# A decoder trunk's ConvFFN: up-projection chunks 2 and 3 as a pair by seven products, and its input sums from other engines

## The chip, the cores and the metric

The kernel runs on one core of one Trainium2 chip. The metric is the device time of one execution in microseconds (us), as the median of several runs. A core has five engines that run at the same time, each through its own list of instructions in order: TensorE (PE; its weight loads are shown as PEld), VectorE (DVE), ScalarE (ACT), GpSimd (POOL) and SyncE (SP, which here issues the loads by DMA). GpSimd issues DMAs too, some of which add what they carry to what stands at the destination.

## The reference

The model has two layers over a residual stream of 512 positions by 1024 features (dilated attention, then forgetting attention). The change touches the ConvFFN that ends each layer:

```python
def conv_ffn(xn, w_up, cw, cb, w_down):      # xn: 512 x 1024, w_up: 1024 x 5632
    a = xn @ w_up
    T = a.shape[1]
    ap = jnp.pad(a, ((0, 0), (CONV_W - 1, 0), (0, 0)))
    a = sum(ap[:, j:j + T] * cw[j] for j in range(CONV_W)) + cb
    gate, val = jnp.split(a, 2, axis=-1)      # 2816 columns each
    return (jax.nn.gelu(gate, approximate=True) * val) @ w_down
...
        f = conv_ffn(rms_norm(h, g[2]), w_up[l], conv_w[l], conv_b[l], w_down[l])
        h = h + rms_norm(f, g[3])
```

## The kernel before

**Precision.** Every operand of a matmul is split into a high part and a low part, and each product is three matmuls (`mm3`, L288 to L290): high by high, high by low, low by high. For the transposed input these are `xbh` and `xbl` (in layer 1 `xch` and `xcl`), for a weight block the two halves of a tile `w`. The high part is a cast on ScalarE. The low part is a subtraction on VectorE (L76 in the class `Weights`, L712 in `Pair.low`), or, where `added` is set (L707, L708), ScalarE writes the negated block and a DMA of GpSimd adds the raw block to it. That DMA is called the accumulating DMA below.

**Up-projection.** Its 5632 columns are worked on as 22 chunks; chunk c has 128 gate and 128 value columns. A chunk's two results (128 columns by 512 positions) stand in two PSUM banks. Then follow the taps of the convolution (`tap`, ScalarE L623 and two operations of VectorE), the GELU (L643 on ScalarE), the product of gate and value (L650), and a store of the result `hc` to `hD` in DRAM (L648, issued by GpSimd one chunk later).

Chunks are computed in one of three ways:

- chunks 0 and 1 by `first_products`, at the boundary from the attention. The transposes of the last two blocks of 128 positions (`bd.transpose(2)` and `(3)`) stand between products over 256 positions (`LO`, `HI`), in banks named `first`;
- chunks 2, 3, 20 and 21 directly by `up`: eight steps of 128 rows, three matmuls of 128x512 each;
- chunks 4 to 19 as eight `Pair`s. A pair's weights are four blocks of 512 rows by 256 columns (A11 and A12 from the gate's columns, A21 and A22 from the value's; A11 and A21 for the first 512 features, A12 and A22 for the others), the input four blocks (two halves of its 1024 features by two halves of the positions). Instead of eight products of blocks it takes seven, of sums of blocks: S1 to S4 are sums of the weight blocks, and `XA` and `XB` (`xsh`, `xsl`) hold sums of the input blocks. A product `p_1` to `p_7` is 24 matmuls of 128x256, for two outputs each. `keep_1`, `keep_7` and `keep_2` copy intermediate results from PSUM (ScalarE, L728), and `sum_1`, `sum_3` and `sum_4` add them (VectorE).

**The sums of the input.** `sums_in` adds `xbh` and `xbl` on GpSimd to get the input in float (L660), forms its four sums on VectorE, and then casts to `xsh` and subtracts to `xsl` (L671, L672).

**Order.** The schedule is written out by hand: each engine gets its instructions in the order of the program. In the loop over pairs an iteration runs the pair's products in the order p_7, p_6, p_4, p_5, p_2, p_3, and the next pair's p_1 stands after p_5. While one pair is multiplied, the next pair's blocks are taken from the list of raw loads (`take`), summed (`s1` to `s4`) and split (`high`, `low`). The A11 of a pair is taken and split another iteration ahead (`n2` in the loop). Ahead of the loop stand `sums_in`, chunks 2 and 3, and the first two pairs' first splits.

**Loads.** `Weights` keeps a list of pieces in the order of use, filled by `add_ffn`. SP issues their loads into `wraw` buffers as far ahead as `ahead` (pieces split ahead of use) and `ahead_dma` (pieces loaded ahead of the split) say; there are ten buffers for these and other tiles of that size.

Of the kernel before, what the change touches and what calls it, by code (L numbers as in the profile page):

```python
# [9 lines left out]
F32 = mybir.dt.float32  # L10
# [3 lines left out]
ALU = mybir.AluOpType  # L14

D = 1024
T = 512
NB = 4
KD = D // 128
HD = 64  # L20
DFF = 2816
# [3 lines left out]
BIG = 3.0e38  # L25


PAIRS = tuple(range(4, 20, 2))
ND = NF // 2
LAST = 3  # L30

# [84 lines left out]
def trunk_kernel(ctx, tc, x, norm_gains, w_qkv_a, w_o_a, w_q_b, w_o_b, kv_norm, w_kvf, b_f,  # L116
                 w_up, conv_w, conv_b, w_down, rope, out):
    nc = tc.nc
    act, dve, pool, pe, sp = nc.scalar, nc.vector, nc.gpsimd, nc.tensor, nc.sync
# [8 lines left out]
    def t8(shape, dt=F32, name="t8"):  # L128
        return p8.tile(shape, dt, tag="t8", name=name)
# [52 lines left out]
    def add_ffn(l):  # L182
        for c in range(NF):
            if c in PAIRS:
                for q, f in ((0, 0), (0, DFF), (1, DFF), (1, 0)):
                    add_block(w_up[l], q, f + c * 128)
            elif c - 1 not in PAIRS:
                add_cols(w_up[l], c * 128)
                add_cols(w_up[l], DFF + c * 128)

        for j in range(ND):
            add(lambda raw, j=j: [(raw[:, 0:512], w_down[l][j * 256:j * 256 + 128, 0:512]),
                                  (raw[:, 512:1024], dT[l][j, :, 0:512])])
            add(lambda raw, j=j: [(raw, dT[l][j, :, 512:1536])])
        add_rows(w_down[l], range(1, NF, 2))
# [26 lines left out]
    W = Weights(nc, new_raw, lambda: t8([128, 2, 1024], F32R, name="w"), pieces)  # L222
# [127 lines left out]
        lo = [t8([128, 4, T], F32R, name=f"{name}l{i}") for i in range(2)]  # L350
        return hi, lo

    def transpose_in(b, xn, xT, between=None):

        pts = []
        for i in range(2):
            pt = bank([128, 4, 128], name="xt_ps")
            for k in range(4):
                pe.transpose(pt[:, k, :], xn[:, (4 * i + k) * 128:(4 * i + k + 1) * 128], ident)
            pts.append(pt)  # L360
        s = slice(b * 128, b * 128 + 128)
        for i, pt in enumerate(pts):
            if i and between is not None:
                between()
            hi, lo = xT[0][i], xT[1][i]
            act.copy(hi[:, :, s], pt)
            dve.tensor_tensor(lo[:, :, s], pt, hi[:, :, s].bitcast(F32), ALU.subtract)

    def xs(xT, kc, s):
        return xT[0][kc // 4][:, kc % 4, s], xT[1][kc // 4][:, kc % 4, s]  # L370
# [8 lines left out]
    ALL, LO, HI = slice(0, 512), slice(0, 256), slice(256, 512)  # L379
# [51 lines left out]
    class Boundary:  # L431
# [26 lines left out]
        def transpose(self, b):  # L458
            if self.xT is None:
                self.xT = new_xT(self.name)  # L460
            transpose_in(b, self.xn.pop(b), self.xT)

    class SharedBoundary(Boundary):

# [76 lines left out]
                self.out(b)  # L541


    def first_products(bd, n):
        bd.norm(3)
        outs = [bank([128, T], name="first") for _ in range(n)]
        ws = []
        for i, o in enumerate(outs):
            ws.append(W.get())
            feat_mm(ws[i], bd.xT, o, LO)  # L550
            if i == 0:
                bd.transpose(2)
# [4 lines left out]
        return outs  # L557


    def load_conv(l):  # L560
# [55 lines left out]
    def ffn(l, bd, cp, nxt, gain, ahead):  # L616
# [36 lines left out]
        xT = None  # L653
        XA, XB = [], []

        def sums_in():

            v = [t8([128, 4, T], name=f"xsum{i}") for i in range(2)]
            for i in range(2):
                pool.tensor_tensor(v[i], xT[0][i].bitcast(F32), xT[1][i].bitcast(F32), ALU.add)  # L660
# [4 lines left out]
            dve.tensor_tensor(v[1][:, :, HI], v[1][:, :, HI], v[0][:, :, LO], ALU.subtract)  # L665
            dve.tensor_tensor(v[1][:, :, LO], v[1][:, :, LO], v[1][:, :, HI], ALU.subtract)
            yield
            for X, src in ((XA, v[0]), (XB, v[1])):
                X += [t8([128, 4, T], F32R, name="xsh"), t8([128, 4, T], F32R, name="xsl")]
                for k in (0, 2):  # L670
                    act.copy(X[0][:, k:k + 2], src[:, k:k + 2])  # L671
                    dve.tensor_tensor(X[1][:, k:k + 2], src[:, k:k + 2], X[0][:, k:k + 2].bitcast(F32), ALU.subtract)  # L672
                    yield
# [4 lines left out]
        class Pair:  # L678
# [206 lines left out]
        def run(steps):  # L885
            for _ in steps:
                pass
# [84 lines left out]
        extra = sums_in()  # L972
        next(extra)
        done, last = Chunk(0, first[0:2]), Chunk(1, first[2:4])
        done.taps()
        next(extra)
        done.product()
        last.taps()
        W.ahead, W.ahead_dma = 1, 3
        W.split(base + 7)  # L980
        W.high_added()
        pairs = [Pair(c) for c in PAIRS]
        p, n = pairs[0:2]

        banks = p.new_banks()
        up(W.get(), banks[0], range(KD))
        for _ in range(3):
            next(extra, None)
        p.take("A11", "A21", "A22")
        p.high("A11", True)  # L990
        p.s1()
        p.s3()
        up(W.get(), banks[1], range(KD))
        run(extra)
        p.high("S1", True)
        done, last = last, Chunk(2, banks)

        banks = p.new_banks()
        up(W.get(), banks[0], range(KD))
        done.product()  # L1000
        last.tap(0)
        p.high("S3")
        p.s2()
        last.tap(1)
        p.high("S2")
        last.gelu()
        p.take("A12")
        p.low("S3")
        p.s4()
        up(W.get(), banks[1], range(KD))  # L1010
        p.high("A22", True)
        p.low("S2")
        last.product()
# [893 lines left out]
```

## Time and profile before

| what | before |
|---|---|
| median of 3 runs | 1103.84 us (1103.52 to 1103.93) |
| profiled execution | 1104.32 us |
| its span | 1102.5 us |
| granted TensorE clock, mean | 0.998 |
| chunks 0 and 1 of layer 0, first matmul to the first of chunk 2 | 178.0 to 202.76 us |
| chunk 2's first matmul to p_1 of chunks 4 and 5, layer 0 | 202.76 to 224.55 us |
| GpSimd's sums of the input, layer 0 | 189.53 us, two of 10.19 us together |

The profile shows one execution. Times in it are counted from the span's start. The span is what the profile covers; the execution's own time lies a little above it. A timeline row gives start, duration, engine, line, operation, tiles, shapes and how many were taken together (x2), and in brackets how long the engine sat idle before it and what released it. Matmuls overlap, so a matmul's row lasts longer than the distance to the next. Layer 1's ConvFFN has the same instructions as layer 0's.

### The profile page before, as it was taken

To read this page: it belongs to the slowest core of one execution; us is meant where nothing else is said; L and a number is where in the kernel's file an instruction comes from. 1 tells how busy PE (TensorE), PEld (TensorE's weight loads), DVE (VectorE), ACT (ScalarE), POOL (GpSimd) and SP (SyncE) were. 2 spreads that over 40 slices of the span, in tenths; PEclk is the share of its full clock that TensorE was granted. 3 is DMA by queue.
4 is the path that set the end of the run, shared out by engine and by line. 5 is a ranking of instruction groups with operands and counts; after the bars stand their busy time and mean duration, and the time that the engine had idled before them with its cause. 6 is when DMAs were issued, how large, how long until landed. Compare 5 with 4: busy or idle time off the path is not lost.

```text
span 1102.5 us, 18986 instructions
## 1 busy us (share of the span) xinstructions
PE 1093.6 (99%) x6905; PEld 968.5 (88%) x6905; DVE 892.3 (81%) x1453; ACT 735.1 (67%) x1232; POOL 231.5 (21%) x335
## 2 busy tenths in 40 slices
PE   9999999999999999999999999999999999999997
PEld 6988889899999988888878888889999999988886
DVE  5897788967887789997698677868967887789994
ACT  6754575777788766576562588856677787856572
POOL 2632001322122211000000545600412122211000
PEclk9999999999999999999999999999999999999999
DMA  9699855499999999793447666783499999998872
GB/s 325 184 356 410 317 174 151 91 227 231 224 224 248 230 295 325 277 338 101 134 153 268 210 159 169 216 265 117 98 224 231 231 221 247 224 296 313 317 249 76
DMA packets 156006, 252.06 MB, mean 229 GB/s; under 512 B 12352, under 2 KB 99384, under 8 KB 155912
## 3 DMA queue, kind: packets, MB, share of 16 engines
q1 hardware_dynamic: 137576, 186.61, 51.1%
q0 software_dynamic: 18336, 64.24, 26.3%
q8 instruction: 54, 0.88, 0.3%
q14 instruction: 40, 0.33, 0.1%
HBM read 166.08 MB, written 39.63 MB: 187 GB/s over the span
## 4 chain that ended last, share of the span: by engine, by line
PE 85%; issue 9%; DVE 2%; ACT 2%; DMA 1%; POOL 1%; DVEq 0%; SPq 0%; POOLq 0%; ACTq 0%
PE up L288 12%; PE up L289 12%; PE up L290 12%; PE acc L288 8%; PE acc L290 8%; PE acc L289 8%; PE qk_ps L289 2%; PE qk_ps L288 2%; PE qk_ps L290 2%; PE s_ps L1733 2%; PE o_ps L1781 2%; PE pT_ps L1766 1%; PE first L290 1%; PE first L288 1%; PE first L289 1%
## 5 line engine op out<-in xcount | busy, mean ns | idle before, releaser
L288 PE MATMUL up<-xsh,w 128*128 128x256 f32 x512 | 144.9, 283 | 0.0
L289 PE MATMUL up<-xsl,w 128*128 128x256 f32 x512 | 144.9, 283 | 0.0
L290 PE MATMUL up<-xsh,w 128*128 128x256 f32 x512 | 144.9, 283 | 0.0
L288 PE MATMUL acc<-w 128*128 128x512 f32 (+1 forms) x311 | 120.7, 388 | 0.3 <-DVE mix L337 0.3
L290 PE MATMUL acc<-w 128*128 128x512 f32 (+1 forms) x311 | 120.6, 388 | 0.1
L705 ACT CAST w<-wraw 128x1024 fp32r<-128x1024 f32 x80 | 82.6, 1048 | 37.7 <-DVE wraw L689 37.7
L624 DVE SCALAR_TENSOR_TENSOR bb<-up,conv,bb 128x511 f32<-128x511 f32 x80 | 59.8, 748 | 57.2 <-ACT bb L623 57.0
L289 PE MATMUL acc<-w 128*128 128x512 f32 (+1 forms) x267 | 103.2, 387 | 0.0
L288 PEld LDWEIGHTS up<-xsh,w 128*128 128x128 f32 x512 | 98.3, 192 | 0.0
L289 PEld LDWEIGHTS up<-xsl,w 128*128 128x128 f32 x512 | 98.3, 192 | 0.0
L290 PEld LDWEIGHTS up<-xsh,w 128*128 128x128 f32 x512 | 98.3, 192 | 0.0
L623 ACT ACTIVATE bb<-up,conv 128x512 f32<-128x512 f32 x80 | 60.2, 780 | 32.7 <-DVE up L775 24.3
L288 PE MATMUL up<-xbh,w 128*128 128x256 f32 (+1 forms) x256 | 80.0, 312 | 0.1
L288 PE MATMUL up<-xch,w 128*128 128x256 f32 (+1 forms) x256 | 80.0, 312 | 0.1
L289 PE MATMUL up<-xbl,w 128*128 128x256 f32 (+1 forms) x256 | 79.2, 310 | 0.0
L289 PE MATMUL up<-xcl,w 128*128 128x256 f32 (+1 forms) x256 | 79.2, 310 | 0.0
L290 PE MATMUL up<-xbh,w 128*128 128x256 f32 (+1 forms) x256 | 79.2, 309 | 0.0
L290 PE MATMUL up<-xch,w 128*128 128x256 f32 (+1 forms) x256 | 79.2, 309 | 0.0
L708 POOL DMA_DIRECT2D w<-wraw x48 | 40.4, 841 | 183.5 <-ACT w L707 96.5
L76 DVE TENSOR_TENSOR w<-wraw,w 128x1024 fp32r<-128x1024 f32 x48 | 65.0, 1376 | 11.9 <-ACT w L58 11.4
L58 ACT CAST w<-wraw 128x1024 fp32r<-128x1024 f32 x62 | 63.7, 1051 | 15.8 <-PE v_ps L289 6.9
L290 PEld LDWEIGHTS acc<-w 128*128 128x128 f32 x311 | 58.4, 188 | 12.9 <-DVE w L817 0.9
(308 smaller groups left out, 3279.6 us busy)
## 6 DMA issues: line engine op xcount, KB each, us to landing
wraw<-in_w_up_dram SPq DMA_DIRECT2D x88, 512.0 KB, 6.6
w<-wraw POOLq DMA_DIRECT2D x62, 512.0 KB, 7.6
dT<-dsums SPq DMA_DIRECT2D x28, 512.0 KB, 7.5
dsums<-in_w_down_dram SPq DMA_DIRECT2D x22, 512.0 KB, 7.5
dsums<-in_w_down_dram SPq DMA_DIRECT2D x44, 256.0 KB, 6.6
hD<-hc POOLq DMA_DIRECT2D x44, 256.0 KB, 7.3
wraw<-dT SPq DMA_DIRECT2D x22, 512.0 KB, 6.8
dact<-hD SPq DMA_DIRECT2D x44, 256.0 KB, 5.3
```

Source lines behind the costliest of these rows:

```text
L58: self.nc.scalar.copy(pair[:, 0], raw)
L76: self.nc.vector.tensor_tensor(pair[:, 1], raw, pair[:, 0].bitcast(F32), ALU.subtract)
L288: pe.matmul(o, ah, bh, start=first, stop=False, skip_group_check=shared)
L289: pe.matmul(o, ah, bl, start=False, stop=False, skip_group_check=shared)
L290: pe.matmul(o, al, bh, start=False, stop=last, skip_group_check=shared)
L623: act.activation(bb[:, s, :], ps, AF.Identity, bias=cp[:, 3, ch:ch + 1], scale=cp[:, 2, ch:ch + 1])
L624: dve.scalar_tensor_tensor(bb[:, s, 1:], ps[:, :T - 1], cp[:, 1, ch:ch + 1], bb[:, s, 1:], ALU.mult, ALU.add)
L705: act.copy(w[:, 0], self.f[key])
L708: pool.dma_start(w[:, 1], self.f[key], accum_op=ALU.add)
L1733: pe.matmul(s[hh][:, :nn], qT[j][:, m, hh, i * 128:(i + 1) * 128], k, start=m == 0, stop=m == 1)
L1766: pe.transpose(o[:, k0 + k, :], p[:, hh, k * 128:(k + 1) * 128], ident)
L1781: pe.matmul(o[64 * hh:64 * hh + 64, i * 128:(i + 1) * 128], Vt[hd // 8][:, k, (hd % 8) * 64:(hd % 8) * 64 + 64], pT[j, i, hh][:, k, :], st ...
```

## The change

`PAIRS` starts at chunk 2, so chunks 2 and 3 become a ninth pair, the first. What stood around the direct chunks is written anew:

- the first pair's blocks are loaded in the order A11, A12, A21, A22, and `W.ahead` and `W.ahead_dma` are set after the first product of chunk 0, so that loads for the pairs are asked for from there on;
- the input in float comes from ScalarE, which copies the transposes of blocks 2 and 3 a second time from PSUM (`plain`, L370), and for blocks 0 and 1 from an addition on VectorE (L565);
- the first pair's p_1 and p_2 run right after `first_products`, and its later products in the loop without p_2;
- its S4 is written over the raw block of A12, and chunk 0's GELU and product come after keep_1;
- the second pair's A11 is taken and split in the loop's iteration 0, after the second tap of chunk 1.

```diff
-PAIRS = tuple(range(4, 20, 2))
+PAIRS = tuple(range(2, 20, 2))
...
-                for q, f in ((0, 0), (0, DFF), (1, DFF), (1, 0)):
+                blocks = (0, 0), (0, DFF), (1, DFF), (1, 0)
+                for q, f in blocks if c > PAIRS[0] else (blocks[0], blocks[3], *blocks[1:3]):
                     add_block(w_up[l], q, f + c * 128)
...
+        def plain(v):
+            for t, pt in zip(v, pts):
+                act.copy(t[:, :, s], pt)
+
+        return plain
...
-    def first_products(bd, n):
+    def first_products(bd, n, begin):
...
             if i == 0:
-                bd.transpose(2)
+                W.ahead, W.ahead_dma = 1, 2
+                plain = bd.transpose(2)
+            if i == 1:
+                begin()
+                v = [t8([128, 4, T], name=f"xsum{i}") for i in range(2)]
+                plain(v)
             if i == 2:
-                bd.transpose(3)
+                for t, hi, lo in zip(v, *bd.xT):
+                    dve.tensor_tensor(t[:, :, LO], hi[:, :, LO].bitcast(F32), lo[:, :, LO].bitcast(F32), ALU.add)
+                bd.transpose(3)(v)
...
-            v = [t8([128, 4, T], name=f"xsum{i}") for i in range(2)]
-            for i in range(2):
-                pool.tensor_tensor(v[i], xT[0][i].bitcast(F32), xT[1][i].bitcast(F32), ALU.add)
-            yield
...
-            def s4(self):
-                self.add("S4", "A12", "S2", ALU.subtract)
+            def s4(self, out=None):
+                self.add("S4", "A12", "S2", ALU.subtract, out)
...
-        base = W.n_get
-        first = first_products(bd, 4)
+        pairs = [Pair(c) for c in PAIRS]
+        p = pairs[0]
+
+        def begin():
+            p.take("A11", "A12")
+            p.high("A11", True)
+
+        first, v = first_products(bd, 4, begin)
         xT = bd.xT
...
-        up(W.get(), banks[0], range(KD))
...
-        up(W.get(), banks[1], range(KD))
...
-        n.take("A11")
-        n.high("A11", True)
-        p.p_1()
-        p.keep_1()
-        prev, m = None, [Chunk(3, banks)]
+        sums = sums_in(v)
+        del v
+        W.ahead_dma = 3
+        p.high("A12", True)
+        p.take("A21", "A22")
+        p.s1()
+        p.s3()
+        done, last = Chunk(0, first[0:2]), Chunk(1, first[2:4])
+        p.high("S3")
+        next(sums)
+        p.s2()
+        next(sums)
+        next(sums)
+        p.high("S2")
+        p.low("S3")
+        next(sums)
+        done.tap(0)
+        next(sums)
+        next(sums)
+        p.low("S2")
+        done.tap(1)
+        p.high("A22", True)
+        p.high("S1", True)
+        p.p_1()
+        p.p_2()
+        p.keep_1()
+        done.gelu()
+        p.s4(p.f["A12"])
+        done.product()
+        prev, m = None, [last]
...
             a.tap(0)
-            p.high("A12", True)
+            if prev:
+                p.high("A12", True)
             p.keep_7()
             p.p_6()
             a.tap(1)
+            if not prev:
+                n.take("A11")
+                n.high("A11", True)
...
-            p.p_2()
+            if prev:
+                p.p_2()
```

Two places show what the engines get. The first is ScalarE in layer 0, from the splits of the first pair's last blocks to the S4 of iteration 0. A row is a line, an operation and its tiles; `L713`, `L715` are the casts and negated copies of weight blocks, `L736` the keep copies, `L635` the taps, `L655` the GELU and its table load. After the change:

```order
L713 CAST w<-wsum 128x1024
L715 ACTIVATE w<-wsum 128x1024
L736 COPY csum<-up 128x256 x2
L655 ACT_TABLE_LOAD
L655 ACTIVATE bb<-bb 128x512
L635 ACTIVATE bb<-first,conv 128x512
L736 COPY csum<-up 128x256 x2
L635 ACTIVATE bb<-first,conv 128x512
L713 CAST w<-wraw 128x1024
L715 ACTIVATE w<-wraw 128x1024
L713 CAST w<-wraw 128x1024
```

The first two rows are S1 of the first pair, and the last split with a negated copy is A11 of the second pair; the last row is S4 (written over A12's raw block). The same place before, from the split of S2 to keep_7 of the pair of chunks 4 and 5 (`L705`, `L707` casts and negated copies, `L728` keeps, `L623` taps, `L643` GELU):

```order
L705 CAST w<-wraw 128x1024
L643 ACTIVATE bb<-bb 128x512
L705 CAST w<-wraw 128x1024
L707 ACTIVATE w<-wraw 128x1024
L705 CAST w<-wraw 128x1024
L707 ACTIVATE w<-wraw 128x1024
L728 COPY csum<-up 128x256 x2
L623 ACTIVATE bb<-up,conv 128x512
L705 CAST w<-wraw 128x1024
L707 ACTIVATE w<-wraw 128x1024
L728 COPY csum<-up 128x256 x2
```

Before, the two splits with negated copies ahead of the first keep are the first pair's A22 and the second pair's A11; the one behind it is A12. After the change, the second pair's A11 stands behind keep_1, the GELU, both taps and keep_7.

The second place is GpSimd in layer 0, from the start of the ConvFFN. Before, its list begins with the sums of the input (`xsum`):

```order
L660 TENSOR_TENSOR xsum_2227<-xbh_1858,xbl_1860 128x2048
L660 TENSOR_TENSOR xsum_2228<-xbh_1859,xbl_1861 128x2048
L96 DMA w<-wraw 128x1024
L708 DMA w<-wraw 128x1024
L708 DMA w<-wsum 128x1024
L648 DMA hD<-hc 128x512
L708 DMA w<-wraw 128x1024
L648 DMA hD<-hc 128x512
```

After the change (`L716` the accumulating DMAs, `L660` the stores of `hc`):

```order
L716 DMA w<-wraw 128x1024 x3
L716 DMA w<-wsum 128x1024
L716 DMA w<-wraw 128x1024
L660 DMA hD<-hc 128x512
L716 DMA w<-wraw 128x1024
L716 DMA w<-wsum 128x1024
```

The sums and one accumulating DMA are gone. The first three rows' DMAs are for the first pair's A11, A12 and A22, the next for its S1, and the third row is the second pair's A11, ahead of the first store to `hD`.

More of the change, by code (lines that the diff above doesn't have):

```diff
@@ L351, in new_xT, with transpose_in @@
         return hi, lo
-    def transpose_in(b, xn, xT, between=None):
+    def transpose_in(b, xn, xT):
         pts = []
@@ L664, in sums_in @@
             yield
-            dve.tensor_tensor(v[1][:, :, HI], v[1][:, :, HI], v[0][:, :, LO], ALU.subtract)
-            dve.tensor_tensor(v[1][:, :, LO], v[1][:, :, LO], v[1][:, :, HI], ALU.subtract)
-            yield
             for X, src in ((XA, v[0]), (XB, v[1])):
+                if src is v[1]:
+                    dve.tensor_tensor(src[:, :, HI], src[:, :, HI], v[0][:, :, LO], ALU.subtract)
+                    dve.tensor_tensor(src[:, :, LO], src[:, :, LO], src[:, :, HI], ALU.subtract)
+                    yield
                 X += [t8([128, 4, T], F32R, name="xsh"), t8([128, 4, T], F32R, name="xsl")]
@@ L967, in up @@
                 mm3(o, wh[:, kc, :], wl[:, kc, :], bh, bl, kc == 0, kc == KD - 1)
-        base = W.n_get
-        first = first_products(bd, 4)
-        xT = bd.xT
[L972 to L985, printed above, removed]
-        up(W.get(), banks[0], range(KD))
[L987 to L990, printed above, removed]
+        pairs = [Pair(c) for c in PAIRS]
[4 more added lines that the diff above has]
+        first, v = first_products(bd, 4, begin)
+        xT = bd.xT
+        sums = sums_in(v)
[3 more added lines that the diff above has]
+        p.take("A21", "A22")
         p.s1()
         p.s3()
-        up(W.get(), banks[1], range(KD))
-        run(extra)
-        p.high("S1", True)
-        done, last = last, Chunk(2, banks)
-        banks = p.new_banks()
-        up(W.get(), banks[0], range(KD))
-        done.product()
[L1001 to L1013, printed above, removed]
-        n.take("A11")
-        n.high("A11", True)
-        p.p_1()
-        p.keep_1()
-        prev, m = None, [Chunk(3, banks)]
+        done, last = Chunk(0, first[0:2]), Chunk(1, first[2:4])
[13 more added lines that the diff above has]
+        p.high("A22", True)
+        p.high("S1", True)
+        p.p_1()
[3 more added lines that the diff above has]
+        p.s4(p.f["A12"])
+        done.product()
+        prev, m = None, [last]
         for i, p in enumerate(pairs):
```

8 lines of the change are left out of this document (3 added, 5 removed).

## The prediction

> **What bounds the kernel now.** I read the page's head, busy shares and chain first, then TensorE's own waits, then the timelines of TensorE, ScalarE, VectorE and GpSimd around the place that changes (178 to 240 us in layer 0).
>
> ```profile
> span 1102.5 us, 18986 instructions
> ...
> PE 1093.6 (99%) x6905; PEld 968.5 (88%) x6905; DVE 892.3 (81%) x1453; ACT 735.1 (67%) x1232; POOL 231.5 (21%) x335
> ...
> PEclk9999999999999999999999999999999999999999
> ...
> PE 85%; issue 9%; DVE 2%; ACT 2%; DMA 1%; POOL 1%; DVEq 0%; SPq 0%; POOLq 0%; ACTq 0%
> ```
>
> TensorE is busy for 99% of the span at the full granted clock, and the chain that ends last is TensorE's work and its issue for 94%. The view of waits says what is left to gain by waiting less:
>
> ```profile
> PE warm L248 <- DVE zero L243: 1.2, 1, 1.2
> PE qk_ps L289 <- DVE w L80: 0.3, 1, 0.3
> PE acc L288 <- DVE mix L337: 0.3, 1, 0.3
> ...
> ```
>
> Columns are the waiting tile and line, the releaser, the sum in us, the count and the mean. No row of TensorE names `up` or `first`: nothing in the up-projection is waited for. So ScalarE, VectorE, GpSimd and the queues cost nothing there now, and the time changes only by the matmuls that TensorE no longer runs, and by stalls that the new order brings in.
>
> **Term 1: TensorE's matmuls.** Chunks 2 and 3 are 96 matmuls of 128x512 in each layer; as a pair they are 7 products of 24 matmuls of 128x256. What follows them (p_1 of the next pair) is one more product in both.
>
> ```profile
> 202.76 0.40 PE L288 MATMUL up<-xbh,w 128*128 128x512 f32 x1
> ...
> 224.55 0.28 PE L288 MATMUL up<-xbh,w 128*128 128x256 f32 x1
> ...
> 227.42 0.28 PE L288 MATMUL up<-xsh,w 128*128 128x256 f32 x1
> ```
>
> Rows give start and duration. From the first direct matmul to p_1 are 224.55 - 202.76 = 21.79 us; p_1 takes 227.42 - 224.55 = 2.87 us to the first p_7. Before: 21.79 + 2.87 = 24.66 us. After: 8 x 2.87 = 22.96 us. **1.70 us less per layer, 3.4 in two**, if nothing waits. A whole pair further on gives a lower gain:
>
> ```profile
> 261.86 0.28 PE L290 MATMUL up<-xbh,w 128*128 128x256 f32 x1
> 262.06 0.39 PE L288 MATMUL up<-xbh,w 128*128 128x256 f32 x1
> ...
> 282.40 0.39 PE L288 MATMUL up<-xbh,w 128*128 128x256 f32 x1
> ```
>
> 282.40 - 262.06 = 20.34 us for the seven products, or 2.91 each, which would make it 24.66 - 8 x 2.91 = 1.4 us. But each such start is late by itself (262.06 follows 261.86 by 0.20 instead of 0.12, and lasts 0.39 instead of 0.28), so that pace holds a small stall; I take 2.87 and put the restart (about 0.15) into term 2.
>
> **Term 2: a new wait, of the second pair's p_1.** Before, a pair's A11 was split an iteration ahead. Now the second pair's A11 is split in iteration 0, behind the first pair's keep_1, GELU, keep_7 and both taps on ScalarE. Its low half comes from a chain: ScalarE's cast, ScalarE's negated copy, GpSimd's accumulating DMA. TensorE reads it at the third matmul of p_1, which stands behind six products: due at 202.76 + 6 x 2.87 + 0.24 = 220.22 us. When it is there follows from these rows of ScalarE:
>
> ```profile
> 198.00 1.28 ACT L643 ACT_TABLE_LOAD   x1
> 199.30 0.63 ACT L643 ACTIVATE bb<-bb 128x512 f32<-128x512 f32 x1
> ...
> 227.89 0.78 ACT L623 ACTIVATE bb<-up,conv 128x512 f32<-128x512 f32 x1
> 228.57 1.05 ACT L705 CAST w<-wraw 128x1024 fp32r<-128x1024 f32 x1
> 229.50 1.06 ACT L707 ACTIVATE w<-wraw 128x1024 fp32r<-128x1024 f32 x1
> 230.46 0.64 ACT L728 COPY csum<-up 128x256 f32<-128x256 f32 x2
> 230.98 0.81 ACT L623 ACTIVATE bb<-up,conv 128x512 f32<-128x512 f32 x1
> 231.65 1.07 ACT L705 CAST w<-wsum 128x1024 fp32r<-128x1024 f32 x1
> ...
> 233.65 0.64 ACT L643 ACTIVATE bb<-bb 128x512 f32<-128x512 f32 x1
> 234.18 1.04 ACT L705 CAST w<-wraw 128x1024 fp32r<-128x1024 f32 x1
> ```
>
> What an instruction holds ScalarE for is the distance to the next start: table load 1.30, GELU 0.53, tap 0.68, cast 0.93, two keep copies 0.52 (0.26 each), tap 0.67. The second keep_1 copy reads a bank that p_2 still writes, so it starts after p_2, whose last matmul starts 0.12 before the next product and lasts 0.28: 202.76 + 2 x 2.87 + 0.16 = 208.66. The sum: 208.66 + 0.26 keep + 1.30 table + 0.53 GELU + 0.68 tap + 0.52 keep_7 + 0.67 tap + 0.93 cast + 1.06 negated copy = 214.61, and 0.30 to GpSimd's issue, by this row (229.50 + 1.06 to 230.86):
>
> ```profile
> 230.86 0.84 POOL L708 DMA_DIRECT2D w<-wraw  x1 [5.89 <-ACT csum L728]
> ```
>
> Issue at 214.9. TensorE doesn't wait if the DMA lands within 220.2 - 214.9 = **5.3 us**. The DMA view (last column: us from issue to landing) has the same transfer at 207.10, 236.48, 264.02, 284.36 and 224.12 us:
>
> ```profile
> w<-wraw POOLq DMA_DIRECT2D x1, 512.0 KB, 4.6
> w<-wraw POOLq DMA_DIRECT2D x1, 512.0 KB, 5.6
> w<-wsum POOLq DMA_DIRECT2D x1, 512.0 KB, 6.4
> w<-wsum POOLq DMA_DIRECT2D x1, 512.0 KB, 8.0
> w<-wraw POOLq DMA_DIRECT2D x1, 512.0 KB, 10.0
> ```
>
> The first had the queue to itself. The last was issued 2.1 us behind another accumulating DMA and right behind the store of hD. Here S1's accumulating DMA goes out at about 208.6, some 6 us ahead, raw blocks that come free load beside it, and a store of hD follows right behind: that is nearest to the third row, 0.5 us ahead of a store and 6 us behind another accumulation. **I take 6.4 us**: it lands at 221.3, 1.1 late, and with the restart of 0.15 the stall is 1.25. Ends: 4.6 gives none, 10.0 gives 4.85.
>
> Beside the rows, a rule: the Trainium skill ("DMA: Bandwidth & Descriptors", section "Anatomy of one DMA — SWDGE (gpsimd) path") fits a GpSimd DMA as about 2.0 us plus its bytes over 436e3 per us. For 512 KB my estimate from that page is 3.2 us, which would land at 218.1 with no stall, and the sum would be term 1 alone. The trace speaks against it for this transfer: even the row that was alone took 4.6, and the sum above goes by the rows.
>
> **What I cost at nothing, and its cover.** The x sums move from GpSimd (two adds) to four ScalarE copies and two VectorE adds:
>
> ```profile
> 189.53 10.19 POOL L660 TENSOR_TENSOR xsum<-xbh,xbl 128x2048 f32<-128x2048 f32 x2 [52.12 <-DVE xbl L367]
> 188.76 1.29 DVE L367 TENSOR_TENSOR xbl<-xt_ps,xbh 128x512 fp32r<-128x512 f32 x2 [0.88 <-ACT xbh L366]
> 190.19 5.04 DVE L76 TENSOR_TENSOR w<-wraw,w 128x1024 fp32r<-128x1024 f32 x1
> 188.14 1.08 ACT L366 CAST xbh<-xt_ps 128x512 fp32r<-128x512 f32 x2 [2.52 <-PE xt_ps L359]
> 194.32 0.78 ACT L623 ACTIVATE bb<-first,conv 128x512 f32<-128x512 f32 x1 [4.16 <-PE first L290]
> ```
>
> GpSimd's 10.19 us go, and with them whatever drew VectorE's L76 out to 5.04 us beside them; TensorE waited for neither, so nothing is gained. A pair of ScalarE copies costs about 1.08 (first pair of casts), and lies in gaps of 2.52 and 4.16 us. It matters whether the sums are early enough:
>
> ```profile
> 207.93 2.35 DVE L672 TENSOR_TENSOR xsl<-xsum,xsh 128x1024 fp32r<-128x1024 f32 x2
> ...
> 210.20 1.22 DVE L689 TENSOR_TENSOR wsum<-wraw 128x1024 f32<-128x1024 f32 x1
> 211.45 1.23 DVE L689 TENSOR_TENSOR wraw<-wraw 128x1024 f32<-128x1024 f32 x1
> ...
> 220.62 1.22 DVE L689 TENSOR_TENSOR wsum<-wraw 128x1024 f32<-128x1024 f32 x1
> 221.75 1.22 DVE L712 TENSOR_TENSOR w<-wraw,w 128x1024 fp32r<-128x1024 f32 x1
> ```
>
> VectorE runs from 190.05 (188.76 + 1.29) through eight passes (s1, s3, two sums, s2, S3's low, two sums; 1.13 to 1.25 each, mean 1.19) and XA's lows (2.35): 190.05 + 9.5 + 2.35 = 201.9. ScalarE then has XB's casts (2 x 0.93), a tap (0.68) and the highs of A22 and S1 (four, 3.8): first keep_1 copy done by 208.5, just ahead of the 208.66 above; at 1.25 a pass, 0.5 later. That 0.5 would add to term 2 and is in the range. p_7 (202.76 + 2 x 2.87 = 208.5) needs XA and S3's low, which VectorE finishes by 199.4: 9 us of cover. p_6 (211.4) needs S2's and XB's lows, about 206.6: 4.8. p_4's low half (due 214.5) comes from A22's accumulation, issued about 206.7: cover 7.8 us against 4.6 to 10.0. p_5's (217.4) from S1's, issued about 208.6: cover 8.8 against the same. p_1 (202.76) and p_2 (205.6) use A11 and A12, accumulated before 193: over 9. A pair behind p_5 waits for keep_2, done about 216.0 against 217.1. Gone from each layer: three of VectorE's lows, four casts, a negated copy and one accumulating DMA; all lay beside TensorE. On SP's queue the requests of the second pair's raw blocks move from the direct chunks to the boundary, before 185, some 27 us ahead of the A11 cast that needs them first (212.6); the longest landing above is 10.0. The later iterations keep their order.
>
> **Sum.** Per layer -1.70 + 1.25 = -0.45; layer 1 runs the same instructions, so -0.9. The profiled execution has 1104.32 us (span 1102.5 and 1.8 around it): 1103.4. It lies 0.48 above the median of the runs shown, 1103.84, from which the forecast is **1102.9**. A measurement of this kernel can tell about 0.2%, 2.2 us, from no change.
>
> **Rivals.**
> - *The DMA is quick and the gain stays.* A landing of 5.7 us or less; 4.6 gives no stall and 1103.84 - 3.4 = 1100.4; 5.6 gives 0.3 + 0.15, 1101.3. For it: 4.6 and 5.6 stand in the rows. Against: these had no store or accumulation close by.
> - *The DMA is slow, slower than before.* The one mechanism is the second pair's A11 queueing at the DMA engines behind S1's accumulation and the early raw loads, with a store behind. It turns the sign where stall exceeds 1.70, a landing over 6.9 us, and passes 0.2% over 8.0: (222.9 - 220.2 + 0.15) = 2.85, so 1103.84 + 2 x 1.15 = 1106.1; 10.0 gives 4.85 and 1110.1. For it: two of the five rows. Against: in those the accumulation ahead was closer than 6 us, or the raw loads more.
> - *Products at 2.91.* The gain is 1.4 per layer; with the stall 1103.5. This lies inside the main case.
>
> On the slow rival, the Trainium skill ("TensorE: Matmul & The Clock Gate", section "Part 1: The HAM clock gate") says that an idle stretch of some 3.4 us halves TensorE's clock for about as long; by that page I estimate another 1.7 us per layer at a stall of 4.85. The rows have no TensorE gap over 1.2 us, and the granted clock is 0.9 or more in all 40 slices, so this trace can't show it.
>
> **How the numbers follow.** Landing 5.7 to 8.0 us, 1101.5 to 1106.1: 0.58, with the forecast in it. Quick: 0.27. Slow: 0.15. The range runs from 1100.4 (no stall) to 1106.3 (8.0 us and a little of ScalarE's lateness) and leaves out the slow tail. Faster by over 0.2% needs a stall under 0.6, so the quick case alone, 0.27; within, 0.58; slower, 0.15.
>
> **What would show it.** In the changed kernel's waits one new row of TensorE, an `up` matmul released by a DMA into `w` or by GpSimd, twice, with 0.5 to 2 us each; from the first p_1 to the second pair's p_1 17.2 us; the landing of the second pair's A11 in the DMA view. A wait at p_7 or p_6 released by VectorE, or at p_4 or p_5 by a DMA, would show my cover wrong; ScalarE's cast of that A11 ending other than near 213.6 would show term 2's chain wrong; a product other than 2.87 us, term 1.

## The result, and the profile after

| what | before | after |
|---|---|---|
| median of 22 runs each | 1103.85 us (1103.36 to 1106.86) | 1105.6 us (1103.31 to 1107.72) |
| ratio to before, 95% interval | | 1.0014 (1.0008 to 1.0021) |
| span of the profiled execution | 1102.5 us | 1104.9 us |
| granted clock, mean | 0.998 | 0.997 |

The change makes the kernel slower by 1.75 us between the medians, and the interval of the ratio leaves out 1. The forecast was 1102.9 us, 0.9 faster, within 1100.4 to 1106.3: the time lies inside that range, but on the other side of no change. The runs also spread more than before.

The page of the changed kernel, its head, busy shares and chain:

```profile
span 1104.9 us, 19361 instructions
...
PE 1092.3 (99%) x7049; PEld 974.3 (88%) x7049; DVE 902.3 (82%) x1477; ACT 752.3 (68%) x1264; POOL 215.9 (20%) x337
...
PE 84%; DVE 5%; DMA 4%; issue 4%; ACT 3%; POOL 1%; SPq 0%; DVEq 0%; POOLq 0%; ACTq 0%
```

TensorE is busy for 1.3 us less, but the span is 2.4 us longer, and DMA has gone from 1% to 4% of the chain. Its view of waits has a new row at its head, the only one on `up`:

```profile
PE up L291 <- DMA w<-wraw: 2.8, 3, 2.2
PE warm L249 <- DVE zero L244: 1.2, 1, 1.2
```

The columns behind the colon are the sum in us, the count and the longest single wait (the prediction read the last as the mean). Two of the three waits, 2.23 us in layer 0 and 0.2 in layer 1, are the third matmul of the second pair's p_1 (L291 is low by high), waiting for the accumulating DMA of A11. The third, 0.44 us, stands at 965.89 us in layer 1's chunk 20, far from the changed part; the kernel before has no such wait there, and why it came was not looked into. TensorE's timeline in layer 0:

```profile
220.86 0.28 PE L290 MATMUL up<-xbl,w 128*128 128x256 f32 x1
223.37 0.39 PE L291 MATMUL up<-xbh,w 128*128 128x256 f32 x1 [2.23 <-DMA w<-wraw]
223.59 0.32 PE L289 MATMUL up<-xbh,w 128*128 128x256 f32 x1
223.71 0.41 PE L290 MATMUL up<-xbl,w 128*128 128x256 f32 x1
...
226.91 0.37 PE L290 MATMUL up<-xbl,w 128*128 128x256 f32 x1
227.12 0.28 PE L291 MATMUL up<-xbh,w 128*128 128x256 f32 x1
```

Two matmuls are 2.51 us apart where 0.12 is usual. Behind the gap, from 223.7 to 227.1, they follow each other by 0.21 instead of 0.12 us. In the view of stretches the reason is the clock (a row gives the stretch, its length and the busy time of TensorE, its weight loads, VectorE, ScalarE and GpSimd; behind these stand the granted clock, the DMA share and GB/s):

```profile
220.28:223.69 3.41, 1.18 (x10) 0.98 (x9) 1.85 (x4) 2.48 (x3) 0.27 (x1) 1.00 1.01 307
223.69:227.10 3.41, 3.41 (x18) 3.41 (x17) 3.31 (x3) 0.85 (x2) 0.83 (x1) 0.50 1.09 243
805.00:805.40 0.40, 0.23 (x2) 0.02 (x1) 0.40 (x2) 0.00 (x0) 0.00 (x0) 1.00 0.95 236
805.40:809.00 3.60, 3.60 (x30) 3.60 (x31) 3.57 (x6) 3.53 (x6) 0.28 (x1) 1.00 1.04 322
```

From 223.69 to 227.10 us, behind the gap of layer 0, TensorE got half its clock; in layer 1, where the gap was 0.46 us, all of it. Eighteen matmuls ran in the 3.41 us of the second row, thirty in the 3.6 us of the fourth. The slow ones cost about 17 x (0.213 - 0.120) = 1.6 us.

Layer by layer, from the first matmul behind `first_products` to the same place in the loop:

```profile
203.46 0.28 PE L289 MATMUL up<-xbh,w 128*128 128x256 f32 x1
...
265.27 0.39 PE L289 MATMUL up<-xbh,w 128*128 128x256 f32 x1
...
787.54 0.28 PE L289 MATMUL up<-xch,w 128*128 128x256 f32 x1
...
845.80 0.39 PE L289 MATMUL up<-xch,w 128*128 128x256 f32 x1
```

Before, this was 262.06 - 202.76 = 59.30 us, in layer 1 as in layer 0. After it is 61.81 in layer 0 (2.51 longer) and 58.26 in layer 1 (1.04 shorter), together 1.47 longer. The rest of the span's 2.4 us lies outside the ConvFFN's changed part: 0.70 before its start in layer 0, where the first 60 us have longer waits of the attention (`qk_ps`) in this execution.

The half clock is not in every run. Of the 22 runs of the changed kernel nine have a mean granted clock of 0.996 or 0.997, which none of the 71 runs of the kernel before beside the experiments has (0.998 or 0.999); the median of the nine is 1106.07 us. Seven have 0.999, and a median of 1104.85. A half clock of 3.41 us takes 0.0015 off the mean, so the six runs at 0.998 can be either.

Why the DMA was late in layer 0, from GpSimd's and SP's timelines and the DMA view of the accumulating DMA issued at 215.80, and of that of layer 1, issued at 800.06:

```profile
215.80 0.84 POOL L716 DMA_DIRECT2D w<-wraw  x1 [5.51 <-ACT w L715]
...
210.10 10.04 SPq L48 DMA_DIRECT2D wraw<-in_w_up_dram  x4
...
w<-wraw POOLq DMA_DIRECT2D x1, 512.0 KB, 7.5
...
w<-wraw POOLq DMA_DIRECT2D x1, 512.0 KB, 5.3
```

Issued within 0.2 us of where the forecast had it (214.9, shifted by the 0.70 of the start), it took 7.5 us in layer 0 and 5.3 in layer 1, where 6.4 was forecast. SP issued four raw loads in 210.1 to 220.1; the trace has them at 210.10, 212.26, 216.26 and 219.78.

### The profile page after: what moved, and what is told of

It is laid out like the page before. It is cut to its first block, busy times and chain, and to the rows that moved or that the text cites. A ratio compares the mean times of both kernels' runs of the same rounds, so it can differ in the third digit from the quotient of the medians.

```text
span 1104.9 us, 19361 instructions
## 1 busy us (share of the span) xinstructions
PE 1092.3 (99%) x7049; PEld 974.3 (88%) x7049; DVE 902.3 (82%) x1477; ACT 752.3 (68%) x1264; POOL 215.9 (20%) x337
## 4 chain that ended last, share of the span: by engine, by line
PE 84%; DVE 5%; DMA 4%; issue 4%; ACT 3%; POOL 1%; SPq 0%; DVEq 0%; POOLq 0%; ACTq 0%
PE up L289 11%; PE up L291 11%; PE up L290 11%; PE acc L289 9%; PE acc L291 9%; PE acc L290 9%; PE qk_ps L290 2%; PE qk_ps L289 2%; PE qk_ps L291 2%; DMA w<-wraw 2%; PE v_ps L289 2%; PE v_ps L291 2%; PE s_ps L1735 2%; PE v_ps L290 2%; PE o_ps L1783 2%
## 5 line engine op out<-in xcount | busy, mean ns | idle before, releaser
L290 PE MATMUL up<-xsl,w 128*128 128x256 f32 x576 | 163.2, 283 | 0.0
L291 PE MATMUL up<-xsh,w 128*128 128x256 f32 x576 | 163.2, 283 | 0.0
L289 PE MATMUL up<-xsh,w 128*128 128x256 f32 x576 | 163.2, 283 | 0.0
L713 ACT CAST w<-wraw 128x1024 fp32r<-128x1024 f32 x92 | 95.2, 1050 | 39.6 <-DVE wraw L697 39.6
L291 PE MATMUL acc<-w 128*128 128x512 f32 (+1 forms) x311 | 120.7, 388 | 0.1
L291 PEld LDWEIGHTS up<-xsh,w 128*128 128x128 f32 x576 | 110.7, 192 | 0.0
L289 PEld LDWEIGHTS up<-xsh,w 128*128 128x128 f32 x576 | 110.7, 192 | 0.0
L290 PEld LDWEIGHTS up<-xsl,w 128*128 128x128 f32 x576 | 110.7, 192 | 0.0
L716 POOL DMA_DIRECT2D w<-wraw x54 | 45.5, 842 | 308.9 <-ACT w L715 198.3
L635 ACT ACTIVATE bb<-up,conv 128x512 f32<-128x512 f32 x80 | 59.9, 778 | 31.6 <-DVE up L783 23.2
L291 PE MATMUL up<-xbh,w 128*128 128x256 f32 (+1 forms) x248 | 74.4, 300 | 2.2 <-DMA w<-wraw 2.2
L289 PE MATMUL up<-xbh,w 128*128 128x256 f32 (+1 forms) x248 | 75.2, 303 | 0.1
L291 PE MATMUL up<-xch,w 128*128 128x256 f32 (+1 forms) x248 | 73.8, 298 | 0.6 <-DMA w<-wraw 0.6
L290 PE MATMUL up<-xbl,w 128*128 128x256 f32 (+1 forms) x248 | 74.4, 300 | 0.0
L289 PE MATMUL up<-xch,w 128*128 128x256 f32 (+1 forms) x248 | 74.4, 300 | 0.0
L290 PE MATMUL up<-xcl,w 128*128 128x256 f32 (+1 forms) x248 | 73.7, 297 | 0.0
L291 PEld LDWEIGHTS acc<-w 128*128 128x128 f32 x311 | 58.4, 188 | 12.8 <-DVE w L825 0.9
L289 PEld LDWEIGHTS acc<-w 128*128 128x128 f32 x311 | 58.4, 188 | 12.6 <-DVE mix L338 0.7
```

What stands on the lines that cost most here:

```text
L289: pe.matmul(o, ah, bh, start=first, stop=False, skip_group_check=shared)
L290: pe.matmul(o, ah, bl, start=False, stop=False, skip_group_check=shared)
L291: pe.matmul(o, al, bh, start=False, stop=last, skip_group_check=shared)
L635: act.activation(bb[:, s, :], ps, AF.Identity, bias=cp[:, 3, ch:ch + 1], scale=cp[:, 2, ch:ch + 1])
L713: act.copy(w[:, 0], self.f[key])
L716: pool.dma_start(w[:, 1], self.f[key], accum_op=ALU.add)
```

## The experiments

All are compared with the kernel before, on the same chip.

**The second pair's A11 with its low half from VectorE.** This takes the DMA out and leaves the order of the rest:

```diff
             if not prev:
                 n.take("A11")
-                n.high("A11", True)
+                n.high("A11")
+                n.low("A11")
```

> Theory (the loss is the second pair's A11 alone: its low half lands 2.4 us late in layer 0, and TensorE then runs at half clock for 3.7 us): with that low half from VectorE instead of the accumulating DMA it is there by about 216.5 us against 220.9, TensorE has no wait on `up`, no stretch of 0.21 us a matmul, and both layers keep term 1's 1.70 us: 1103.85 - 3.4 = 1100.4 (1100.0 to 1101.2). Rival A (the seven products don't gain 1.70 us a layer, or the boundary costs it elsewhere): the wait goes, but the time stays at 1102.5 or above. Rival B (VectorE, with 1.2 us more in that iteration, is late for the next thing): a new wait on VectorE at p_3 or at the second pair's p_7, 1101.5 to 1104.

Measured: 1101.18 us (1100.80 to 1101.61, 8 runs), ratio 0.9974 (0.9963 to 0.9984). No row of TensorE's waits names `up`. VectorE and TensorE:

```profile
214.67 1.22 DVE L720 TENSOR_TENSOR w<-wraw,w 128x1024 fp32r<-128x1024 f32 x1
...
202.79 0.28 PE L289 MATMUL up<-xbh,w 128*128 128x256 f32 x1
...
225.84 0.28 PE L289 MATMUL up<-xsh,w 128*128 128x256 f32 x1
...
240.34 0.39 PE L289 MATMUL up<-xbh,w 128*128 128x256 f32 x1
...
260.67 0.38 PE L289 MATMUL up<-xbh,w 128*128 128x256 f32 x1
```

The low half is ready by 215.9, and the loss is gone with that one DMA; so rivals A and B fall. The same rows give the true size of term 1. Eight products take 225.84 - 202.79 = 23.05 us against 24.66 before: 1.61, at 2.88 a product rather than 2.87. To 260.67 it is 57.88 against 59.30: 1.42. The other 0.19 is one more late start: each pair behind the first has one, at 240.34 as at 260.67 (about 0.1 late, and lasting 0.39 us), and now there is a pair more.

**Split earlier on ScalarE, the DMA kept.**

```diff
         p.keep_1()
+        n = pairs[1]
+        n.take("A11")
+        n.high("A11", True)
         done.gelu()
...
-            if not prev:
-                n.take("A11")
-                n.high("A11", True)
```

> The accumulating DMA stays, but ScalarE splits the second pair's A11 right behind keep_1, ahead of the table load and the GELU. Theory (the place on ScalarE made the DMA late): issue at about 212.1 us, 8.8 us ahead of the third matmul of p_1; with a landing of 5.3 to 8.4 us no wait: 1100.4 to 1101.0, with at most 0.5 us more a layer where keep_7, 1.9 us later, holds p_4 (due at 214.9). Rival (whatever is issued there lands late since S1's accumulation and the raw loads hold the DMA engines until 223): a landing of over 9 us, a wait again, and 1103 or more.

Measured: 1106.16 us (1105.03 to 1108.80, 9 runs), ratio 1.0021 (1.0011 to 1.0030). The rival was right in layer 0 (the last row is from the waits):

```profile
211.72 0.84 POOL L716 DMA_DIRECT2D w<-wraw  x1 [1.69 <-ACT w L715]
...
w<-wraw POOLq DMA_DIRECT2D x1, 512.0 KB, 11.4
...
220.59 0.28 PE L290 MATMUL up<-xbl,w 128*128 128x256 f32 x1
223.16 0.39 PE L291 MATMUL up<-xbh,w 128*128 128x256 f32 x1 [2.29 <-DMA w<-wraw]
223.38 0.28 PE L289 MATMUL up<-xbh,w 128*128 128x256 f32 x1
...
PE up L289 <- DVE up L778: 0.9, 1, 0.9
```

Issued four microseconds earlier, it landed at 223.1, as late as in the changed kernel (223.3). So in layer 0 the place on ScalarE, on which the forecast spent its arithmetic, didn't decide when the DMA was done. In layer 1 it took 8.0 us and was in time, but TensorE waited 0.90 us for VectorE further on, at 824.49 us (the last row), for a reason that was not looked into; chunk 20's wait is there too. And the gap of 2.57 us left the clock whole in this execution; three of the nine runs have a mean clock of 0.997.

**The other part of the change alone**: the kernel before with the sums of the input from ScalarE's `plain` copies and VectorE. The edit is the change's own in `transpose_in`, `first_products` and `sums_in`, and nothing else of it.

> The kernel before with only the other part of the change: the sums of the input from ScalarE's float copies and VectorE instead of GpSimd, chunks 2 and 3 still direct. Theory (that part lies beside TensorE): 1103.85 within 0.5 us, no new wait of TensorE, and VectorE's L76 beside it shrinks from 5.04 to about 1.2 us. Rival A (the copies hold the banks of the transposes or ScalarE is late for the taps): TensorE waits at `first`, 0.5 us or more slower. Rival B (GpSimd's additions cost something): 0.5 us or more faster.

Measured: 1104.44 us (1104.09 to 1104.61, 11 runs), ratio 1.0003 (0.9994 to 1.0012). No new wait of TensorE, and none at `first`. In the changed sums' place VectorE's low reads

```profile
193.47 1.23 DVE L76 TENSOR_TENSOR w<-wraw,w 128x1024 fp32r<-128x1024 f32 x1 [1.60 <-ACT w L58]
```

instead of 5.04 us beside GpSimd's additions. A saving of that size beside TensorE is worth nothing here, as forecast.

**Raw loads held back.** A DMA of 64 bytes on SP reads from A11's low half and so waits until the accumulating DMA has landed; the third pair's raw loads stand behind it:

```diff
                 n.high("A11", True)
+                sp.dma_start(held[0:1, 0:16], n.t["A11"][0:1, 1, 0:16].bitcast(F32))
             if n:
                 n.take("A21", "A22")
```

> The changed kernel with one more DMA on SP, of 64 bytes out of the second pair's A11, that can't start until its accumulating DMA has landed; SP's loads of the third pair's raw blocks (512 KB each, issued at 210.1, 212.3 and 216.3 us before) stand behind it. The accumulating DMA is issued where it was, at about 215.8. Theory (those loads hold the DMA engines, so the landing time hardly depends on the issue): it now lands in 4.5 to 5.5 us, by 221.3 at the latest against 220.9, the wait is 0 to 0.5 us, no half clock, and the time is 1100.8 to 1102.0. Rival (it queues behind S1's accumulating DMA, issued 6.3 us ahead): it lands in 7 us or more as before, and the time stays at 1105 to 1106.5. Rival B (the loads, 5 us and more later, are missed by the third pair): a new wait further on, 0.5 to 3 us a layer.

Measured: 1105.94 us (1105.42 to 1107.15, 11 runs), ratio 1.0018 (1.0009 to 1.0027). The landing and the price of holding, in GpSimd's timeline, the DMA view and the waits:

```profile
208.74 0.83 POOL L717 DMA_DIRECT2D w<-wsum  x1 [1.05 <-ACT csum L737]
215.10 0.84 POOL L717 DMA_DIRECT2D w<-wraw  x1 [5.52 <-ACT w L716]
...
w<-wraw POOLq DMA_DIRECT2D x1, 512.0 KB, 4.5
...
PE up L291 <- DVE w L721: 2.7, 2, 1.3
...
PE up L289 <- DVE up L779: 1.1, 2, 0.6
```

S1's accumulating DMA is still 6.4 us ahead and the store of hD right behind, yet A11 lands in 4.5 us in both layers, and its wait is gone. So without the loads S1's DMA alone doesn't make it late; it is itself done by then (5.4 us instead of 6.7, landed at 214.1). The kernel gains nothing, since later waits on VectorE take the place of that one (rival B): up to 1.3 us at the second pair's p_7 and 0.6 further on, in each layer. Ahead of them VectorE sat idle for 2.82 us behind a ScalarE cast, and ScalarE for 1.57 us behind a late raw load; which of the two set the waits was not taken apart.

**S1's accumulating DMA taken away**, its low half by VectorE, the loads kept:

```diff
-        p.high("S1", True)
+        p.high("S1")
+        p.low("S1")
         p.p_1()
```

> The other suspect taken away: the first pair's S1 gets its low half from VectorE, so that no accumulating DMA is issued between A22's (207.6) and that of the second pair's A11; the raw loads stay and the one that waited for S1's landing comes earlier. If the loads are what holds the DMA: the landing of A11 stays over 6.5 us in layer 0, and the time at 1103.5 to 1107. If S1's accumulating DMA is: 4.5 to 5.5 us and 1100.8 to 1102.

Measured: 1102.59 us (1100.78 to 1105.12, 10 runs), ratio 0.9987 (0.9978 to 0.9996). A11's landing by the DMA view, layer 0 and layer 1:

```profile
w<-wraw POOLq DMA_DIRECT2D x1, 512.0 KB, 4.9
...
w<-wraw POOLq DMA_DIRECT2D x1, 512.0 KB, 5.4
```

By the landing S1's DMA would be the cause; the time lies between the two ranges. But its removal also moves a load: the raw block that waited for the buffer of S1's sum goes out at 212.19, 3.0 us ahead of A11's DMA, and no longer at 216.26, 0.46 behind it. So I asked for that load alone.

**One load held.** The small DMA stands behind the first two loads, so only the one that S1's landing releases is kept until A11 has landed:

```diff
                 n.high("A22", True)
+                if not prev:
+                    sp.dma_start(held[0:1, 0:16], n.t["A11"][0:1, 1, 0:16].bitcast(F32))
                 n.p_1()
```

> The changed kernel with the small DMA on SP again, now behind two of the three loads: only the load that S1's landing releases (issued at 216.3, 0.5 us behind the second pair's A11) waits for A11's landing; those at 210.1 and 212.3 go as before. If that one load, right behind the accumulating DMA, is what delays it: A11 lands in 4.5 to 5.5 us in layer 0, no wait over 0.5 us, no half clock, and 1101 to 1103 with something for the later load. If the two earlier loads delay it: over 6.5 us in layer 0, a gap over 1.5 us, and 1104.5 or more.

Measured: 1103.17 us (1102.43 to 1104.70, 11 runs), ratio 0.9996 (0.9987 to 1.0005).

```profile
w<-wraw POOLq DMA_DIRECT2D x1, 512.0 KB, 6.2
...
PE up L291 <- DMA w<-wraw: 0.9, 1, 0.9
```

Neither end was hit: 6.2 us in layer 0, a gap of 1.19 us, whole clock. Of the 3.0 us by which 7.5 exceeds 4.5, the load right behind makes 1.3. The other 1.7 took both the two loads ahead and S1's DMA: without the loads it was 4.5, without S1's DMA 4.9. The DMA view of the changed kernel shows how they act together. Its rows give a queue's packets, MB and share of the engines; q0 is GpSimd's queue and q1 is SP's. First 210.2 to 215 us, while S1's DMA is under way, then 215.8 to 218, from A11's issue on:

```profile
q0 software_dynamic: 200, 0.75, 98.8%
q1 hardware_dynamic: 96, 0.10, 7.5%
...
q1 hardware_dynamic: 830, 0.83, 107.7%
q0 software_dynamic: 1, 0.00, 0.0%
```

Beside S1's DMA the two loads issued at 210.10 and 212.26 hardly move. When it is through they do, and A11's DMA moves nothing until 218.2, 2.4 us behind its issue (1.4 us where all loads are held). From A11's issue to its landing SP's queue moved 1.55 MB in the changed kernel's layer 0 (7.5 us), 0.83 with the one load held (6.2), 0.41 without S1's DMA (4.9) and none with all loads held (4.5). In layer 1 of the changed kernel it was 0.53 MB in 5.3 us, with the nearest load 1.4 us behind. The order isn't strict: layer 1 of other runs has 0.86 to 0.89 MB in 5.4 to 6.3 us.

**Waits of set size.** VectorE computes the second pair's A11 low half behind `sum_3`, three, four or five times over (the same values each time), so that TensorE waits without any DMA:

```diff
-                n.high("A11", True)
+                n.high("A11")
...
             p.sum_3()
+            for _ in range(0 if prev else 4):
+                n.low("A11")
```

> A wait of set size, with no DMA in it: the second pair's A11 low half is computed by VectorE three times over, behind sum_3, so that p_1's third matmul waits about 2.6 us in both layers. Theory (an idle stretch of about that length is what halves the clock): in both layers matmuls at about 0.21 us for 3 to 4 us behind the wait, so that a layer loses 2.6 + 1.6 and gains 1.7: about 1108.9. Rival (the half clock needs 3.4 us of idleness, or came from the DMA traffic at that moment): matmuls at 0.12 us right behind the wait, about 1105.7.

> VectorE's low half four times over: TensorE waits about 3.0 us at p_1's third matmul in both layers. So far gaps between two matmuls of 1.95 (twice) and 2.57 us left the clock whole, and one of 2.51 us halved it. If a window that runs freely decides (a gap halves the clock where it takes up most of one window): half clock in one layer or both, by chance. If a fixed length decides, the two layers agree.

> The same five times over: a wait of about 4.2 us in both layers. Both theories of a clock gate: half clock in both layers, 3 to 4 us long, some 1.6 us more each. If neither shows it, the half clock of the changed kernel did not come from the idle stretch.

Single times: 1106.47, 1110.36 and 1113.85 us. The stretches behind the gap, layer 0 and layer 1 of the three in that order (granted clock in the third column from the right):

```profile
222.00:227.00 5.00, 4.95 (x41) 4.95 (x42) 4.97 (x6) 3.83 (x6) 0.58 (x1) 1.00 0.62 139
...
804.70:809.00 4.30, 4.23 (x35) 4.23 (x36) 4.27 (x7) 3.12 (x5) 0.00 (x0) 1.00 0.45 93
```

```profile
224.28:227.69 3.41, 3.41 (x18) 3.41 (x18) 3.38 (x5) 3.41 (x6) 0.18 (x1) 0.50 0.34 93
...
807.96:811.37 3.41, 3.41 (x17) 3.41 (x18) 3.38 (x5) 2.41 (x3) 0.00 (x0) 0.50 0.10 18
```

```profile
224.50:230.00 5.50, 5.42 (x33) 5.42 (x34) 5.31 (x7) 4.20 (x6) 0.83 (x1) 0.69 0.33 103
...
810.60:816.50 5.90, 5.88 (x30) 5.88 (x31) 5.26 (x6) 3.99 (x6) 0.85 (x1) 0.55 0.37 104
```

The gaps came out shorter than aimed at in the first (1.95 us twice, whole clock; so that run couldn't settle it) and came to 3.21 and 4.47 us in the others, with half clock in all four layers. The DMA share is lower there than in the changed kernel, so idleness, not traffic, halves the clock. 16 or 17 slow matmuls (1.5 to 1.6 us) follow in three of the four, and 24 (2.4 us) in the last, whose clock was already down during the gap.

The granted clock also shows what decides between gaps of like length. Every half-clock stretch behind a gap lasts 3.41 us (the last one twice that), and in the run with four passes the two start 583.68 us apart, 171 times 3.413: the clock changes only on the edges of such windows. In the changed kernel's profile an edge at 223.69 stands 877.23 us ahead of the drop at the end, 1100.92. The early split drops at 1099.67 there, which puts an edge at 222.44, inside its gap of 2.57 us:

```profile
219.04:222.45 3.41, 1.83 (x16) 1.63 (x14) 3.35 (x6) 0.82 (x2) 0.85 (x1) 1.00 1.03 278
222.45:225.86 3.41, 2.70 (x22) 2.70 (x23) 2.62 (x3) 2.58 (x4) 0.84 (x1) 1.00 1.08 259
```

TensorE was idle for 1.58 us of the one window and 0.71 of the next, and kept its clock. The changed kernel's gap lay in one window, 3.41 - 1.18 = 2.23 us of it idle, and the next window ran at half clock. So did the next window in all seven cases with 2.18 us or more idle in one. In none of those with up to 1.67 (the gaps of 1.95 us) was the clock lowered; only a window that was already at half clock kept it for one more with 1.57 us idle, in the last run's layer 1. Where between 1.67 and 2.18 the limit lies no run shows.

**The changed kernel twice more.**

> The changed kernel as it is, once more. If half clock by chance and a landing time that varies make its spread (1103.31 to 1107.72): in each layer a gap at p_1's third matmul between 0.3 and 2.6 us, and half clock only where the gap is over 2 us; a layer without half clock stands at -1.42 plus its gap against before, one with it 1.6 higher. If something else makes the spread, the span doesn't follow from the two gaps and the half-clock stretches within 0.5 us.

> The changed kernel again: the same as for the run ahead of it, as a second sample of both layers.

Single times: 1106.44 and 1105.60 us. In layer 0 the DMA took 7.5 us both times, the gap was 2.46 and 2.47 us, and the clock behind it

```profile
222.00:227.00 5.00, 4.99 (x29) 4.99 (x30) 3.58 (x3) 1.97 (x4) 0.83 (x1) 0.66 1.07 245
```

```profile
222.00:227.00 5.00, 5.00 (x29) 5.00 (x30) 3.59 (x3) 1.84 (x4) 0.83 (x1) 0.66 1.06 240
```

with 16 and 17 slow matmuls. In layer 1 the gaps were 0.87 and 0.48 us, at the whole clock. The spans, 1104.6 and 1103.8 us, fit the expectation's sum to 0.5 us. So layer 0's gap is no accident: the three profiles have it within 0.05 us. That all three have the half clock is partly luck, by the mean clocks of the 22 runs above. The first of the two also shows a wait that the result's profile doesn't have: in layer 1 TensorE waited 0.32 us at p_5 for S1's accumulating DMA, which took 8.8 us.

**Both low halves on VectorE**: the first and the fifth edit together.

> Low halves of the first pair's S1 and of the second pair's A11 both by VectorE. If the wait on A11 was all, this is the same as A11's alone, 1101.2 within 0.5 us. If two more passes of 1.2 us are too many for VectorE there, a wait on VectorE at the second pair's p_7 or p_3, 0.5 us or more. If S1's accumulating DMA still cost something elsewhere, 1100.7 or less.

Measured: 1100.87 us (1100.68 to 1101.24, 9 runs), ratio 0.9973 (0.9963 to 0.9982): the same as A11's alone, and no wait of TensorE on `up`. By their medians either version beats both kernels, the one before by about 3 us and the changed one by 4.4 to 4.7.

## Why the prediction was wrong, by its steps

- **Bound: right.** TensorE sets the end, and the new row of its waits on `up` is the one that was named: the second pair's p_1, on the accumulating DMA. It was to be 0.5 to 2 us in each layer and was 2.23 and 0.2.
- **Term 1, 1.70 us less per layer: mis-sized.** 1.42 measured (1.61 by the products at 2.88 us, less 0.19 for one more late start). I had the lower figure of 1.4 from the pace of a whole pair and set it aside as a small stall of its own; it was that, and the added pair pays it too.
- **Term 2, when the DMA is issued: right.** Forecast 12.2 us behind the first p_1, measured 12.3 (215.80 - 203.46). But the run that split A11 earlier shows that this hardly mattered in layer 0.
- **Term 2, "I take 6.4 us": the first step that failed.** 7.5 us in layer 0 in three of three profiles, 5.3 to 6.3 in layer 1. I chose the row by its distance to the nearest accumulation and store. What decides is all that moves beside it, the raw loads above all: held back, the same DMA takes 4.5 us; the one load right behind it costs 1.3. Nor were the five rows the whole of the record: of the 18 accumulating DMAs that the kernel before issues from 207 to 292 us, nine took over 6.9 us, the landing from which the forecast itself had the sign turn. The slow rival named the loads, but set its chance at 0.15 and its onset at 8.0 us.
- **Term 2, "with the restart of 0.15 the stall is 1.25": the second, and the larger one.** The restart is 0.1 only while the clock holds. Behind 2.51 us it was 1.6 in the profiled executions. Layer 0 therefore had -1.42 + 2.39 + 1.6 = +2.6 (rows: +2.51), layer 1 -1.42 + 0.34 = -1.1 (rows: -1.04); the sum of +1.5 stands against +1.75 between the medians. The forecast had -0.45 for each. So of the 2.4 us between its -0.9 and the rows' +1.47 the half clock makes 1.6 and term 1 0.6; the two stalls make only 0.2, since layer 1's was as much shorter than 1.25 as layer 0's was longer. Runs without half clock are still about 1 us above the kernel before (median 1104.85), and no profile caught one: what they lose beside layer 0's gap stays open.
- **The half clock belonged into the main case.** I put it into the slow rival at a stall of 4.85 us. The Trainium skill ("TensorE: Matmul & The Clock Gate", section "Part 1: The HAM clock gate") has the clock drop after an idle window of some 3.4 us, by a window that runs freely. The traces agree on the window (half-clock stretches of 3.41 us, edges that fall anywhere in a gap) and differ on the length: a gap of 2.46, 2.47 or 2.51 us inside one window was enough, one of 2.57 across an edge was not, 1.95 never was (two layers), and from 3.21 on all four were. A stall of 1.25, as forecast, would have been safe by these rows; one of 2.4 depends on where the window stands, as the nine of 22 runs show.
- **Costs at nothing: right but for p_5.** The sums alone are 1.0003 (0.9994 to 1.0012). In the result's profile no wait stands at p_7, p_6, p_4 or p_5. In one of the two further profiles p_5 waited 0.32 us for S1's DMA, whose 8.8 us used up the cover of 8.8.
- **The quick rival** (1100.4, no stall) is what the versions without that DMA measure, 1100.9 to 1101.2, its gain smaller by the two times 0.28 us of term 1.

## What to carry to other kernels

When a change moves a transfer close to its deadline, read its duration from rows with the same loads beside it: a buffer that comes free at that moment starts a load, and that load competes with it. A stall of over 2 us on TensorE may cost another 1.6 us in half clock (here where 2.18 us or more fell into one window of 3.41), so price it as more than its length, and as a chance. Where a late transfer's work fits into an engine with slack (one pass of 1.2 us here), moving it there can be worth more than moving it earlier.

## What had not been expected of the hardware

- The same accumulating DMA of 512 KB took 4.5 us with SP's loads held back, 4.9 to 8.0 with them, and 11.4 where it stood 2.5 us behind S1's and two loads were issued 0.3 and 2.4 us behind it: issued four microseconds earlier, it landed no sooner.
- The half clock starts only at the edge of the window: behind the gap of 3.21 us in layer 0 the first matmuls still ran at 0.12 us, from 223.15 on, and at 0.21 only behind the edge at 224.28.
